# A decoder block with product-key experts: dense path moved to the middle four chunks, last selections moved into the dense loop

## Chip, cores and metric

One NeuronCore of a Trainium2 chip runs the whole kernel as one program. The metric is the device time of one execution in microseconds (us); lower is better. PE is the matrix engine, DVE the vector engine, ACT the scalar engine, POOL the GpSimd engine and SP the engine that issues most of the DMAs. The kernel is written for a planner: Python emits instructions in a program order, the planner plays them through a model of the chip and fixes from that the order of each engine's own queue. Where two instructions are ready, the one that was emitted earlier goes first. On the chip every engine then works through its queue strictly in that order.

## What is computed

A token sequence (16 meta tokens and 1024 tokens, width 1024) goes through a convolution branch beside causal attention, then through a product-key expert layer, then a final norm. Only the expert layer matters here. Per token it picks 8 x 16 of 16384 experts and mixes them:

```python
q = (xb @ wq).reshape(C, PEER_HEADS, 2, PEER_DK_HALF)
s = jnp.einsum('chpd,hpnd->chpn', q, keys).astype(jnp.float32)
sv, si = lax.top_k(s, K)                                    # 16 of 128 keys, twice per head
cand = sv[:, :, 0, :, None] + sv[:, :, 1, None, :]
cidx = si[:, :, 0, :, None] * N_KEYS + si[:, :, 1, None, :]
top_s, sel = lax.top_k(cand.reshape(C, PEER_HEADS, K * K), K)
eidx = jnp.take_along_axis(cidx.reshape(C, PEER_HEADS, K * K), sel, axis=-1)
g = jax.nn.softmax(top_s, axis=-1)
u = u_tab[eidx]
act = jax.nn.gelu(jnp.einsum('chkd,cd->chk', u, xb).astype(jnp.float32), approximate=False)
w = (g * act).astype(xb.dtype)
return jnp.einsum('chk,chkd->cd', w, v_tab[eidx])
```

## The kernel before

The 1024 tokens are 8 chunks of 128, in five sets: set 0 is chunk 0, set 1 chunk 1, set 2 chunks 2 and 3, set 3 chunks 4 and 5, set 4 chunks 6 and 7. ORDER (L61) is the program order of the middle of the kernel. B is the attention of a set (`attend`), C its output projection, expert queries and first top-16 (`mix_out`), S its second top-16 with the indices and weights (`select`), T the turning of these so that tokens lie along the free axis (`turn`), E one chunk's expansion of its weights into a table g_d in memory (`expand`), X, Y, N and U open pools, transpose the dense chunks and start the first three dense steps, G32 takes 32 gather steps, D0 is the dense loop (`dense`).

The expert layer is done in two ways. **Gathered chunks** (GATHER, 0 to 3): 128 tiles of 512 KB are fetched from u_tab (tile ug, L687, 3 buffers), each reduced on DVE against the tokens (ujunk, L690), and 128 from v_tab (tile vg, L713, 7 buffers), each four of them used by 16 matmuls (gv, L717). This makes 2 x 4 x 128 = 1024 tiles. `gather_all` runs them in rounds of steps of four tiles: u of chunk 0; then v of chunk 0 beside u of the next; and so on; v of the last alone, 160 steps in all. **Dense chunks** (DENSE, 4 to 7): 128 steps i1, each the product of 512 tokens with 128 experts (pa, 24 matmuls with split operands), Gelu, weighting by g_d (gt, L817), splitting into wh and wl, and after every four steps the product with v_tab (pv, 96 matmuls). In the dense loop 1.1 gather steps are emitted per i1 (RATE), so that v of the second gathered chunk is emitted from i1 = 29 on. The planner may take emitted work earlier when nothing emitted before it can use the engine; tile pools that are opened late (those of `dense` after the ones of `expand` and `select` are closed) hold their work back until the memory is free.

`select` is a chain between two engines: DVE makes eq (L636), POOL multiplies it into ep (L637), DVE reduces ep (L638), 16 times per chunk. `expand` is one too: DVE makes two, one and ah (L752 to L754), every second al is made by POOL (L755), PE multiplies, ACT copies out (st, L763).

Of the kernel before, what the change touches and what calls it, by code (L numbers as in the profile page):

```python
# [13 lines left out]
F32 = mybir.dt.float32  # L14
F32R = mybir.dt.float32r
# [20 lines left out]
H = 8  # L36
# [23 lines left out]

ORDER = "B1 C1 S1 B2 C2 T1 S2 B3 C3 T2 S3 B4 X0 C4 T3 E0 E1 Y0 S4 T4 E2 N0 E3 U3 G32 D0"  # L61
RATE = 1.1
CONV_POOL = [3]
GATHER = [0, 1, 2, 3]
DENSE = [4, 5, 6, 7]
ND = len(DENSE) * P
# [16 lines left out]
def trunk_kernel(ctx, tc, x, meta, g_mix, w_ab, w_lat, g_q, w_uq, g_kv, w_ukv, conv_w, conv_b,  # L83
# [468 lines left out]
    def mix_out(si, MT):  # L552
# [22 lines left out]

        sv = [sel.tile([P, H, 2, TK], F32, name=f"sv{si}_{j}", tag="sv", bufs=dim.nw) for j in range(nt)]
        sx = [sel.tile([P, H, 2, TK], U32, name=f"sx{si}_{j}", tag="sx", bufs=dim.nw) for j in range(nt)]
        for h in range(H):
# [29 lines left out]

    def select(c, sv, sx):
        si = sel.tile([P, H, 2, TK], F32, name=f"si{c}", tag="sif", bufs=1)  # L610
        V.tensor_copy(si, sx)
# [12 lines left out]
        ti = sel.tile([P, H, TK], U32, name=f"ti{c}", tag="ti", bufs=1)  # L624
        for h in range(H):
            top16(tv[:, h], ti[:, h], cand[:, h], NCAND)
        tf = sel.tile([P, H, TK], F16, name=f"tf{c}", tag="tf", bufs=1)
        V.tensor_copy(tf, ti)
        e = sel.tile([P, H, TK], F32, name=f"ef{c}", tag="ef", bufs=dim.nw)
        for h in range(0, H, HB):  # L630
            for i, n in enumerate((NC1, NCAND)):
                ks = slice(8 * i, 8 * i + 8)
                sh = [P, HB, n, 8]
                eq = sel.tile(sh, F16, name=f"eq{c}_{h}_{i}", tag=f"eq{i}", bufs=2)
                pr = sel.tile(sh, F32, name=f"ep{c}_{h}_{i}", tag=f"ep{i}", bufs=2)
                V.tensor_tensor(eq, tf[:, h:h + HB, None, ks].broadcast_to(sh), iota_c[:, None, :n].broadcast_to(sh), op=OP.is_equal)  # L636
                G.tensor_tensor(pr, eq, cidx[:, h:h + HB, :n, None].broadcast_to(sh), op=OP.mult)  # L637
                V.tensor_reduce(e[:, h:h + HB, ks], pr.rearrange("p h c k -> p h k c"), axis=AX.X, op=OP.add)  # L638
        g = sel.tile([P, H, TK], F32, name=f"gg{c}", tag="gg", bufs=dim.nw)
        gs = sel.tile([P, H], F32, name=f"gs{c}", tag="gs", bufs=1)  # L640
# [15 lines left out]
    def turn(c):  # L656

        ef, g = picks[c]
        tp = bank(f"et{c}", (P, 4, P), "s" if c in DENSE else "c")
        transpose_to(tp[:, 0], ef, P)  # L660
        eT = const.tile([P, P], I32, name=f"eT{c}", tag="eT", bufs=5)
        V.tensor_copy(eT, tp[:, 0])
        if c in GATHER:
            chunks[c] += (eT,)
        else:
            transpose_to(tp[:, 1], g.rearrange("p h k -> p (h k)"), P)
            t = sel.tile([P, 4, P], F16, name=f"gd{c}", tag="gd", bufs=len(DENSE))
            A.activation(t[:, 0], tp[:, 1], AF.Copy, scale=GSCALE)
            V.scalar_tensor_tensor(t[:, 1], tp[:, 1], GSCALE, t[:, 0], op0=OP.mult, op1=OP.subtract)
            ii = sel.tile([P, 2, P], I32, name=f"ii{c}", tag="ii", bufs=1)  # L670
            V.tensor_scalar(ii[:, 0], eT, 7, None, op0=OP.logical_shift_right)
            V.tensor_scalar(ii[:, 1], eT, NK - 1, None, op0=OP.bitwise_and)
            V.tensor_copy(t[:, 2:4], ii)
            chunks[c] = t
# [20 lines left out]
    def gather_v(c):  # L695
# [27 lines left out]
        V.tensor_tensor(ht, ht, acc, op=OP.add)  # L723
        finish(c, ht)

# [6 lines left out]

    def finish(c, ht):
        r = inv_rms(ht, f"o{c}")
        V.scalar_tensor_tensor(ht, ht, r, gfin, op0=OP.mult, op1=OP.mult)  # L735
        nc.scalar.dma_start(out[c * P:(c + 1) * P], ht)
# [49 lines left out]
    def dense_u(i1, bank):  # L786
# [9 lines left out]
        return ge  # L796

    def dense():
        dn = ctx.enter_context(tc.tile_pool(name="dn", bufs=1, **RW))
        psd = ctx.enter_context(tc.tile_pool(name="psd", bufs=1, space=PSUM, **RW))  # L800

        def pbank(name):
# [6 lines left out]
        for g in range(NK // NG):  # L809
# [3 lines left out]
            for b in range(NG):  # L813
                i1 = NG * g + b
                ge = ges.pop(0) if ges else dense_u(i1, pbank)
                gev = ge.rearrange("p (a t) -> p a t", t=TG)
                V.tensor_tensor(gev, gev, gt[:, :, b], op=OP.mult)  # L817
                wh = dn.tile([P, ND], F32R, name=f"wh{i1}", tag="wh", bufs=5)
                wl = dn.tile([P, ND], F32R, name=f"wl{i1}", tag="wl", bufs=4)
                A.activation(wh, ge, AF.Copy)  # L820
                V.tensor_tensor(wl, ge, wh.bitcast(F32), op=OP.subtract)  # L821
                W.append((wh, wl))
                while done < RATE * (i1 + 1):
                    next(steps, None)
                    done += 1
# [9 lines left out]
        for _ in steps:  # L835
            pass
        for ci, c in enumerate(DENSE):
            finish(c, acc[:, ci])

    dim = SimpleNamespace(nw=1, nk=1, wraw=WRAW0)  # L840
    al_ctx, cp_ctx, bp_ctx, ex_ctx, sel_ctx, ps_ctx = [ctx.enter_context(ExitStack()) for _ in range(6)]
# [29 lines left out]
    for t in tops[0]:  # L871
        select(*t)
        turn(t[0])
    for _ in front:
        pass
    for c_ in (bp_ctx, cp_ctx, sel_ctx, ps_ctx, al_ctx):
        c_.close()
    dim = SimpleNamespace(nw=NW, nk=NC, wraw=WRAW)
    psv = ctx.enter_context(tc.tile_pool(name="psv", bufs=1, space=PSUM, **RW))
    ps = ps_ctx.enter_context(tc.tile_pool(name="ps", bufs=1, space=PSUM, **RW))  # L880
    open_banks(ps, c=2, b=2, s=2)
    gp = ctx.enter_context(tc.tile_pool(name="gp", bufs=1, side="right", **RW))
    sel = select_pool()
    cp, gffn = mix_pool("left")
    bp, k_m, v_m, goa = attend_pool("right")
    gfin = load_bcast(gp.tile([P, D], F32, name="gfin"), g_fin)
    wd = [gp.tile([P, 4, 8 * 32], F32, name=f"wd{q}") for q in range(2)]
# [3 lines left out]
    for step in ORDER.split():  # L891
# [5 lines left out]
        elif step[0] == "S":  # L897
            for t in tops[i]:
                select(*t)
        elif step[0] == "T":  # L900
# [7 lines left out]
        elif step[0] == "Y":  # L908
            cp_ctx.close()
            dx = ctx.enter_context(tc.tile_pool(name="dx", bufs=1, **RW))  # L910
            XD = (dx.tile([P, KD, ND], F32R, name="xdh"), dx.tile([P, KD, ND], F32R, name="xdl"))
            du = ctx.enter_context(tc.tile_pool(name="du", bufs=1, **RW))
            ges = []
        elif step[0] == "N":
            dense_x()
        elif step[0] == "U":
            ges += [dense_u(k, lambda n: bank(n)) for k in range(i)]
        elif step[0] == "E":
            expand(i)
        elif step[0] == "D":  # L920
            ex_ctx.close()
            sel_ctx.close()
            ps_ctx.close()
            dense()
        else:
            for _ in range(i):
                next(steps)
# [54 lines left out]
```

## Time and profile before

| | |
|---|---|
| time, median of 3 runs | 3044.03 us (3032.12, 3044.03, 3045.99) |
| profiled execution, its own time | 3022.82 us |
| span of the profile | 3021.0 us |
| busy: PE / DVE / POOL / ACT | 86% / 71% / 52% / 33% |
| moved by DMA | 858 MB, 284 GB/s over the span |

The span is the time from the first to the last instruction; the execution's own time holds 1.8 us more. A busy share over the whole span mixes stages: the first 1400 us have many short waits between engines, the rest is the dense loop, in which PE has hardly a gap.

### The profile page before, as it was taken

The page shows a single profiled execution, that of the slowest core. Times are in us where ns is not written, and L with a number is a line of the kernel's source. Part 1 is how long each engine was busy: PE and PEld are TensorE (multiplying, and loading weights), DVE is VectorE, ACT ScalarE, POOL GpSimd, SP SyncE. Part 2 cuts the span into 40 slices and gives each one's busy share as a digit, 9 for nine tenths or more (in the row PEclk, how much of TensorE's full clock was granted, in tenths as well). Part 3 has the DMA queues.
Part 4 walks back from the last instruction along what each step waited for, and adds up shares of the span by engine and source line. Part 5 has one row for each costly group of instructions (what it writes and reads, how often), then busy time and mean ns, then how long its engine had stood idle before and what let it go on. Part 6 is the DMA issues. An engine that isn't in the chain of part 4 may idle for free. (4 is left out here: it accounts for less than half of the span.)

```text
span 3021.0 us, 40497 instructions
## 1 busy us (share of the span) xinstructions
PE 2592.5 (86%) x13295; PEld 1928.7 (64%) x13295; DVE 2158.9 (71%) x4917; ACT 1010.7 (33%) x2200; POOL 1572.4 (52%) x1608
## 2 busy tenths in 40 slices
PE   7788668897886755556999999999999999999998
PEld 6775446676653533334877777777777777776665
DVE  4789857989998999775887866666666666643333
ACT  6435425352430333342232222222222222222222
POOL 5885443534568667663343454544554445434443
PEclk9888859898898877667999999999999999999999
DMA  5014689897788996998888899999999999988996
GB/s 159 29 49 150 216 256 317 263 294 237 241 318 292 335 314 208 325 296 300 308 289 288 297 374 331 343 343 348 335 340 342 348 333 343 338 287 313 320 321 229
DMA packets 372563, 858.36 MB, mean 284 GB/s; under 512 B 37952, under 2 KB 134400, under 8 KB 368256
## 3 DMA queue, kind: packets, MB, share of 16 engines
q0 software_dynamic: 147456, 536.94, 50.8%
q1 hardware_dynamic: 216528, 295.68, 29.1%
q10 hardware_dynamic: 8368, 23.15, 2.1%
q8 instruction: 105, 1.72, 0.2%
q14 instruction: 106, 0.87, 0.1%
HBM read 798.92 MB, written 56.71 MB: 283 GB/s over the span
## 5 line engine op out<-in xcount | busy, mean ns | idle before, releaser
L713 POOL DMA_INDIRECT vg<-in_dram,eT x512 | 563.0, 1100 | 635.7 <-PE gv L717 504.3
L687 POOL DMA_INDIRECT ug<-in_dram,ei x512 | 545.5, 1065 | 605.4 <-DVE ujunk L690 328.9
L690 DVE SCALAR_TENSOR_TENSOR ujunk<-ug,xn 128x1024 bf16<-128x1024 f32 x512 | 640.6, 1251 | 144.2 <-DMA ug<-in_dram,ei 140.8
L834 DVE TENSOR_TENSOR acc<-acc,pv 128x512 f32<-128x512 f32 x256 | 171.5, 685 | 204.7 <-PE pv L178 204.2
L717 PE MATMUL gv<-vg,wd 128*32 128x512 f32 x2048 | 272.2, 649 | 24.8 <-DMA vg<-in_dram,eT 24.5
L178 PE MATMUL pv<-v_0h,wh 128*128 128x512 f32 x512 | 201.2, 398 | 26.5 <-ACT wh L820 20.1
L178 PE MATMUL pa<-xdh,u_0h 128*128 128x512 f32 x512 | 202.0, 395 | 5.6 <-ACT st L763 4.2
L178 PE MATMUL pv<-v_1l,wh 128*128 128x512 f32 x512 | 201.2, 395 | 5.5 <-DVE v_1l L783 5.5
L178 PE MATMUL pa<-xdl,u_0h 128*128 128x512 f32 x512 | 201.3, 393 | 0.0
L178 PE MATMUL pv<-v_0l,wh 128*128 128x512 f32 x512 | 201.1, 396 | 0.0
L178 PE MATMUL pa<-xdh,u_1h 128*128 128x512 f32 x512 | 201.1, 393 | 0.0
L178 PE MATMUL pa<-xdh,u_1l 128*128 128x512 f32 x512 | 200.7, 392 | 0.4 <-DVE u_1l L783 0.3
L178 PE MATMUL pa<-xdh,u_0l 128*128 128x512 f32 x512 | 200.8, 392 | 0.0
L178 PE MATMUL pa<-xdl,u_1h 128*128 128x512 f32 x512 | 200.1, 391 | 0.3 <-DVE xdl L192 0.3
L178 PE MATMUL pv<-v_1h,wl 128*128 128x512 f32 x512 | 200.0, 393 | 0.0
L782 ACT ACTIVATE u_1h<-u_1r 128x512 fp32r<-128x512 f32 x128 | 80.7, 631 | 350.4 <-PE pa L178 346.2
L178 PE MATMUL pv<-v_1h,wh 128*128 128x512 f32 x512 | 196.0, 395 | 0.0
L178 PE MATMUL pv<-v_0h,wl 128*128 128x512 f32 x512 | 194.8, 395 | 1.0 <-DVE wl L821 1.0
L763 ACT ACTIVATE st<-pg 128x256 f32<-128x256 f32 x256 | 128.6, 646 | 200.7 <-PE pg L761 157.7
L782 ACT ACTIVATE u_0h<-u_0r 128x512 fp32r<-128x512 f32 x128 | 80.8, 631 | 322.9 <-PE pa L178 320.6
L783 DVE TENSOR_TENSOR u_0l<-u_0r,u_0h 128x512 fp32r<-128x512 f32 x128 | 90.0, 703 | 118.6 <-ACT u_0h L782 114.6
L760 PE MATMUL pg<-ah,two 128*128 128x128 f16 x512 | 97.1, 269 | 82.7 <-DVE ah L754 60.2
(449 smaller groups left out, 5887.5 us busy)
## 6 DMA issues: line engine op xcount, KB each, us to landing
g_d<-st SPq DMA_DIRECT2D x32, 1024.0 KB
u_0r<-in_dram SPq DMA_DIRECT2D x128, 256.0 KB
u_1r<-in_dram SPq DMA_DIRECT2D x128, 256.0 KB
gt<-g_d SPq DMA_DIRECT2D x32, 1024.0 KB
v_0r<-in_dram SPq DMA_DIRECT2D x128, 256.0 KB
v_1r<-in_dram SPq DMA_DIRECT2D x128, 256.0 KB
wo<-in_dram SPq DMA_DIRECT2D x80, 256.0 KB
wq<-in_dram SPq DMA_DIRECT2D x80, 256.0 KB
```

Of the source, the lines that this page charges most:

```text
L178: PE.matmul(dst, l, r, start=first and j == 0, stop=last and j == 2)
L687: G.indirect_dma_start(out=ug, out_offset=None, in_=u_tab, in_offset=bass.IndirectOffsetOnAxis(ap=ei[:, j:j + 1], axis=0))
L690: V.scalar_tensor_tensor(junk, ug, 1.0, xn, op0=OP.mult, op1=OP.mult, accum_out=dots[:, j:j + 1])
L713: G.indirect_dma_start(out=vg[j], out_offset=None, in_=v_tab, in_offset=bass.IndirectOffsetOnAxis(ap=eT[:, t:t + 1], axis=0))
L717: PE.matmul(acc[32 * j:32 * j + 32, 512 * n:512 * n + 512], w[:, j, 32 * i:32 * i + 32], vg[j][:, 512 * n:512 * n + 512], start=q == 0 and ...
L760: PE.matmul(pg[:, k], two[:, a, :, b], ah[:, a, :, b], start=True, stop=False)
L763: A.activation(st[i][:, :, r0 + r:r0 + r + 4].rearrange("p a b -> p b a"), pg[:, :, i * NK // 2:(i + 1) * NK // 2], AF.Copy, scale=1.0 / G ...
L782: A.activation(hi, raw, AF.Copy)
L783: V.tensor_tensor(lo, raw, hi.bitcast(F32), op=OP.subtract)
L834: V.tensor_tensor(a, a, pv, op=OP.add)
```

## The change

Chunks 2 to 5 become the dense ones, chunks 0, 1, 6 and 7 the gathered ones. ORDER changes: the expansions E0 to E3 stand ahead of C4, and S4 and T4 are gone from it. `select` becomes a generator with eight yields; inside `dense` a generator `late_set` runs `select` and `turn` of chunks 6 and 7, one slice after each i1, so that chunk 6 is emitted by i1 = 8 and chunk 7 by i1 = 16. What these slices need gets a pool of its own (late) and a new sel pool in the dense phase, with single instead of double buffers; the turned tables gd move to the pool of `expand`; ef and gg get four buffers before the dense loop. To make room, g_final is no longer held: it is loaded into a vg buffer once for each gathered chunk and once for the dense ones, and wh has four instead of five buffers. In the dense loop `turn` takes one of the three PSUM banks of pa.

```diff
-ORDER = "B1 C1 S1 B2 C2 T1 S2 B3 C3 T2 S3 B4 X0 C4 T3 E0 E1 Y0 S4 T4 E2 N0 E3 U3 G32 D0"
+ORDER = "B1 C1 S1 T1 B2 C2 S2 B3 C3 S3 B4 X0 T2 T3 E0 E1 E2 E3 C4 Y0 N0 U3 G32 D0"
-GATHER = [0, 1, 2, 3]
-DENSE = [4, 5, 6, 7]
+GATHER = [0, 1, 6, 7]
+DENSE = [2, 3, 4, 5]
+LATE = 4
...
+        pool = late if si == LATE else sel
+        sv = [pool.tile([P, H, 2, TK], F32, name=f"sv{si}_{j}", tag="sv", bufs=dim.nw) for j in range(nt)]
...
         for h in range(H):
+            if h % 2 == 0:
+                yield
             top16(tv[:, h], ti[:, h], cand[:, h], NCAND)
+        yield
...
-        e = sel.tile([P, H, TK], F32, name=f"ef{c}", tag="ef", bufs=dim.nw)
+        e = sel.tile([P, H, TK], F32, name=f"ef{c}", tag="ef", bufs=dim.sp)
         for h in range(0, H, HB):
+            if h and h % 2 == 0:
+                yield
...
-                eq = sel.tile(sh, F16, name=f"eq{c}_{h}_{i}", tag=f"eq{i}", bufs=2)
-                pr = sel.tile(sh, F32, name=f"ep{c}_{h}_{i}", tag=f"ep{i}", bufs=2)
+                eq = sel.tile(sh, F16, name=f"eq{c}_{h}_{i}", tag=f"eq{i}", bufs=dim.sb)
+                pr = sel.tile(sh, F32, name=f"ep{c}_{h}_{i}", tag=f"ep{i}", bufs=dim.sb)
...
-        tp = bank(f"et{c}", (P, 4, P), "s" if c in DENSE else "c")
+        tp = bank(f"et{c}", (P, 4, P), "c")
...
-        finish(c, ht)
+        finish(c, ht, load_bcast(gp.tile([P, D], F32, name=f"gfin{c}", tag="vg", bufs=7), g_fin))
...
+    def late_set():
+        for t in tops[LATE]:
+            for _ in select(*t):
+                yield
+            turn(t[0])
+
     def dense():
...
+        banks["c"] = (psd, 3, "act")
+        rest = late_set()
...
-                wh = dn.tile([P, ND], F32R, name=f"wh{i1}", tag="wh", bufs=5)
+                wh = dn.tile([P, ND], F32R, name=f"wh{i1}", tag="wh", bufs=4)
...
                 W.append((wh, wl))
+                next(rest, None)
                 while done < RATE * (i1 + 1):
                     next(steps, None)
                     done += 1
...
+        gfin = load_bcast(gp.tile([P, D], F32, name="gfin", tag="vg", bufs=7), g_fin)
         for ci, c in enumerate(DENSE):
-            finish(c, acc[:, ci])
+            finish(c, acc[:, ci], gfin)
...
+    late = ctx.enter_context(tc.tile_pool(name="late", bufs=1, side="right", **RW))
...
-    gfin = load_bcast(gp.tile([P, D], F32, name="gfin"), g_fin)
...
             sel_ctx.close()
             ps_ctx.close()
+            dim.sb = dim.sp = 1
+            sel = ctx.enter_context(tc.tile_pool(name="sel", bufs=1, side="right", **RW))
             dense()
```

## Rows read from the trace of the kernel before

**Rows 1.** The page's second part: busy tenths in 40 slices of the span.

```profile
PE   7788668897886755556999999999999999999998
DVE  4789857989998999775887866666666666643333
```

**Rows 2.** Stages: each engine's busy time (instructions), granted clock, DMA share, GB/s.

```profile
1110.00:1205.00 95.00, 52.90 (x325) 33.26 (x324) 92.91 (x261) 30.82 (x59) 73.08 (x83) 0.70 0.75 249
1205.00:1395.00 190.00, 105.78 (x741) 67.14 (x739) 129.66 (x195) 71.93 (x144) 118.72 (x91) 0.64 0.92 300
1395.00:1725.00 330.00, 298.34 (x1278) 240.68 (x1280) 263.41 (x445) 93.32 (x164) 121.71 (x111) 0.96 0.86 301
1725.00:2995.00 1270.00, 1267.49 (x6213) 913.98 (x6208) 731.09 (x1176) 353.88 (x593) 603.51 (x560) 1.00 0.92 331
```

**Rows 3.** The same stages, POOL's fetches of u tiles alone (L687).

```profile
1205.00:1395.00 190.00, 37.90 (x31) 0.64 0.92 300
1395.00:1725.00 330.00, 121.20 (x110) 0.96 0.86 301
1395.00:3021.00 1626.00, 314.21 (x289) 0.99 0.90 322
```

**Rows 4.** The same, POOL's fetches of v tiles alone (L713).

```profile
1205.00:1395.00 190.00, 42.61 (x40) 0.64 0.92 300
1395.00:1725.00 330.00, 0.51 (x1) 0.96 0.86 301
1395.00:3021.00 1626.00, 409.51 (x378) 0.99 0.90 322
```

**Rows 5.** Groups by line, 1110 to 1205 us: busy, mean ns, idle before.

```profile
L638 DVE TENSOR_REDUCE ef<-ep 128x8 f32<-128x160 f32 (+1 forms) x29 | 18.3, 644 | 0.0
L636 DVE TENSOR_TENSOR eq<-tf,iota_c 128x160 f16<-128x160 f16 (+1 forms) x32 | 14.3, 470 | 0.0
L619 DVE TENSOR_TENSOR cand<-sv 128x32 f32<-128x32 f32 (+3 forms) x11 | 3.6, 393 | 0.0
L604 DVE FIND_INDEX8 ti<-tv,cand 128x8 uint32<-128x50 f32 x16 | 3.0, 196 | 0.0
...
L637 POOL TENSOR_TENSOR ep<-eq,cidx 128x160 f32<-128x160 f16 (+1 forms) x32 | 26.6, 853 | 11.4 <-DVE eq L636 11.3
...
L763 ACT ACTIVATE st<-pg 128x256 f32<-128x256 f32 x36 | 18.2, 643 | 36.6 <-PE pg L761 30.2 <-DMA g_d<-st 6.4
L795 ACT ACT_TABLE_LOAD x1 | 1.3, 1283 | 0.0
```

**Rows 6.** Groups by line, 1205 to 1395 us.

```profile
L763 ACT ACTIVATE st<-pg 128x256 f32<-128x256 f32 x136 | 68.3, 647 | 112.4 <-PE pg L761 89.1 <-DMA g_d<-st 10.9 <-DVE ht L735 6.9
...
L753 DVE TENSOR_TENSOR one<-io,gd 128x1024 f16<-128x1024 f16 x33 | 22.6, 685 | 38.4 <-POOL al L755 38.3
```

**Rows 7.** Groups by line, 1395 to 1725 us, DVE's largest.

```profile
L690 DVE SCALAR_TENSOR_TENSOR ujunk<-ug,xn 128x1024 bf16<-128x1024 f32 x111 | 135.6, 1222 | 50.5 <-DMA ug<-in_dram,ei 49.2 <-DMA xn<-xn_d 0.7
```

**Rows 8.** Waits of 1395 to 1725 us: total, times, longest.

```profile
POOL ug L687 <- DVE ujunk L690: 189.9, 95, 13.5
...
ACT wh L820 <- PE pv L178: 16.8, 5, 12.3
```

**Rows 9.** Timeline near the end, POOL and PE: start, duration, instruction, idle before.

```profile
2960.45 0.94 POOL L713 DMA_INDIRECT vg<-in_dram,eT  x1 [4.21 <-PE gv L717]
2961.70 0.95 POOL L713 DMA_INDIRECT vg<-in_dram,eT  x1 [0.30 <-issue]
...
2969.37 1.19 POOL L713 DMA_INDIRECT vg<-in_dram,eT  x1 [4.17 <-PE gv L717]
...
2976.11 1.92 PE L717 MATMUL gv<-vg,wd 128*32 128x512 f32 x16
...
3009.44 0.39 PE L178 MATMUL pv<-v_1h,wl 128*128 128x512 f32 x1
```

**Rows 10.** DMA issues: count, median us from issue to landing.

```profile
vg<-in_dram,eT POOLq DMA_INDIRECT x512, 6.3
```

More of the change, by code (lines that the diff above doesn't have):

```diff
@@ L574, in mix_out @@
             to_T(hs[j], P, NT, j * P)
-        sv = [sel.tile([P, H, 2, TK], F32, name=f"sv{si}_{j}", tag="sv", bufs=dim.nw) for j in range(nt)]
-        sx = [sel.tile([P, H, 2, TK], U32, name=f"sx{si}_{j}", tag="sx", bufs=dim.nw) for j in range(nt)]
+        pool = late if si == LATE else sel
+        sv = [pool.tile([P, H, 2, TK], F32, name=f"sv{si}_{j}", tag="sv", bufs=dim.nw) for j in range(nt)]
+        sx = [pool.tile([P, H, 2, TK], U32, name=f"sx{si}_{j}", tag="sx", bufs=dim.nw) for j in range(nt)]
         for h in range(H):
@@ L638, in select @@
                 V.tensor_reduce(e[:, h:h + HB, ks], pr.rearrange("p h c k -> p h k c"), axis=AX.X, op=OP.add)
-        g = sel.tile([P, H, TK], F32, name=f"gg{c}", tag="gg", bufs=dim.nw)
+        g = sel.tile([P, H, TK], F32, name=f"gg{c}", tag="gg", bufs=dim.sp)
         gs = sel.tile([P, H], F32, name=f"gs{c}", tag="gs", bufs=1)
@@ L666, in turn @@
             transpose_to(tp[:, 1], g.rearrange("p h k -> p (h k)"), P)
-            t = sel.tile([P, 4, P], F16, name=f"gd{c}", tag="gd", bufs=len(DENSE))
+            t = ex.tile([P, 4, P], F16, name=f"gd{c}", tag="gd", bufs=len(DENSE))
             A.activation(t[:, 0], tp[:, 1], AF.Copy, scale=GSCALE)
             V.scalar_tensor_tensor(t[:, 1], tp[:, 1], GSCALE, t[:, 0], op0=OP.mult, op1=OP.subtract)
-            ii = sel.tile([P, 2, P], I32, name=f"ii{c}", tag="ii", bufs=1)
+            ii = ex.tile([P, 2, P], I32, name=f"ii{c}", tag="ii", bufs=1)
             V.tensor_scalar(ii[:, 0], eT, 7, None, op0=OP.logical_shift_right)
@@ L731, in gather_all, with finish @@
             streams = [gather_v(c) for c in GATHER[k:k + 1]] + [gather_u(c) for c in GATHER[k + 1:k + 2]]
-    def finish(c, ht):
+    def finish(c, ht, gfin):
         r = inv_rms(ht, f"o{c}")
@@ L836, in dense @@
             pass
+        gfin = load_bcast(gp.tile([P, D], F32, name="gfin", tag="vg", bufs=7), g_fin)
         for ci, c in enumerate(DENSE):
-            finish(c, acc[:, ci])
-    dim = SimpleNamespace(nw=1, nk=1, wraw=WRAW0)
+            finish(c, acc[:, ci], gfin)
+    dim = SimpleNamespace(nw=1, nk=1, wraw=WRAW0, sb=2, sp=1)
     al_ctx, cp_ctx, bp_ctx, ex_ctx, sel_ctx, ps_ctx = [ctx.enter_context(ExitStack()) for _ in range(6)]
@@ L871, in trunk_kernel @@
     for t in tops[0]:
-        select(*t)
+        list(select(*t))
         turn(t[0])
@@ L877, in trunk_kernel @@
         c_.close()
-    dim = SimpleNamespace(nw=NW, nk=NC, wraw=WRAW)
+    dim = SimpleNamespace(nw=NW, nk=NC, wraw=WRAW, sb=2, sp=4)
     psv = ctx.enter_context(tc.tile_pool(name="psv", bufs=1, space=PSUM, **RW))
@@ L898, in trunk_kernel @@
             for t in tops[i]:
-                select(*t)
+                list(select(*t))
         elif step[0] == "T":
```

## Prediction

> **What bounds the kernel now.** Read the busy tenths first [rows 1]: PE is at 9 or more from slice 19 on, about 1395 us, and below that before. The span has two parts, and they must be costed apart.
>
> *Before 1395 us* no engine is full for long. The windows [rows 2] show DVE nearly full, 92.9 of 95 us, from 1110 to 1205 us, where `select` of chunks 6 and 7 runs, and 129.7 of 190 us after it, where only E2 and E3 are left. In that second stretch DVE waits 38.3 us for POOL's al [rows 6], which stands behind fetches in POOL's queue. This part ends when the last st is copied.
>
> *From 1395 us* PE carries the end: 298 of 330 us, then 1267 of 1270 us at a granted clock of 1.00, the upper of its two levels [rows 2]. But it does not stand alone. The gather stream runs beside it for the whole time: 289 + 378 = 667 of the 1024 tiles are fetched after 1395 us [rows 3, 4], and its last matmuls end only some microseconds before the last pv at 3009.4 us [rows 9]. So two chains end together, PE's and the gather's. A change that starts the dense loop earlier helps only as far as the gather gets as much done in the shorter time.
>
> The gather has three paces. From 1205 to 1395 us: 71 tiles in 190 us, 0.37 per us. From 1395 to 1725 us u tiles alone, 110 in 330 us, plus one v: v of chunk 1 is emitted from i1 = 29 on, and PE has older work until then. From 1725 to 2995 us the rest, 667 - 111 = 556 tiles in 1270 us, 2.28 us each [rows 2 to 4].
>
> **The change part by part.**
>
> *Out of the first part.* `select` of two chunks leaves it. DVE: eq 14.3, 32 reductions of 0.64 = 20.6, five steps of top-16 of about 3.0 each = 15, candidates twice 3.6: close to 60 us with small ones [rows 5]. POOL: 26.6 us for ep. The stretch took 95 us, but E made 36 of its 256 copies in it, and at the pace of the next stretch (136 in 190 us, 1.4 us each) these need 50 us of their own [rows 5, 6]. So at least 95 - 50 = 45 us go. At most the 95 us go: E's part of the stretch would then fit into the 60 us in which DVE is idle in the next one [rows 2]. Moving E ahead of C4 lets C4's top-16 fill that idle time in place of the fetch-bound work, so I stand nearer to the upper end: 80 us, dense loop from 1315 us.
>
> *What the gather loses by that.* 80 us at 0.37 tiles per us are 30 tiles. POOL gets 26.6 us back, at most 21 tiles at one issue per 1.25 us [rows 9]; DVE is wanted by others, so I credit 10. At 1315 us 357 - 30 + 10 = 337 tiles are done; before, at 1395 us, 1024 - 667 = 357.
>
> *Into the dense loop.* 60 us of DVE enter the first 16 or so i1, about 180 us, ahead of the u fetches in program order. DVE was 263 of 330 us busy there, and of its idle 67 us 49 were waits for a u tile to land [rows 2, 7]; POOL in turn waited 190 us for DVE to free u buffers [rows 8]. So DVE is the pace of the u stream. A u tile costs 1.22 us of DVE [rows 7]. If the select takes all its time from ujunk, 60 / 1.22 = 49 tiles go; if it fills all the idle time of those 180 us (a fifth, 37 us), 23 / 1.22 = 19 go. I take 30. In the first 330 us 111 - 30 = 81 tiles are fetched instead of 111. Single buffers of eq and ep make each of 32 hand-overs wait for POOL's queue; dense splits stand behind them on DVE, and behind those PE. That is the reason not to take 19.
>
> *PE.* Its work is the same except for some 10 more v tiles after the start: 1.92 us per four [rows 9], 5 us. Without the gather it would end at 3010 - 80 + 5 = 2935 us, less 0.48 us for each tile left to the end.
>
> *Small edits.* g_final costs 4 more loads of 512 KB and, with ht, holds a second vg buffer at each chunk's end, on SP's queue ahead of later weights: between nothing and one four-tile step (9 us, 2960.45 to 2969.37 [rows 9]) each, so 0 to 36; I take 8, since the weights are loaded ahead. One wh buffer less makes ACT wait for pv; that wait was 16.8 us in 330 before [rows 8], and ACT is busy 93 of 330 [rows 2]: 0 on the path, and if its cover goes, the splits behind wh are late by as much again. Exp between Gelus reloads tables, at most four loads of 1.3 us [rows 5] on the same idle ACT: 0. The two late turns hold one of three pa banks for a transpose: 0.
>
> *The sum.* At 1315 + 330 = 1645 us 337 + 81 = 418 tiles are done; 606 are left, with the 8 us for g_final worth 610. At 2.28 us each PE's dense work ends at 2908 us with 57 tiles left: (2908 - 1645) / 2.28 = 553, and 2935 - 57 x 0.48 = 2908. Then v tiles are fetched alone. Before, four of them took 9 us (2.28 a tile), which is what seven buffers give when a tile lands 6.3 us after its issue [rows 9, 10]: 0.95 + 6.3 + 1.92 = 9.2. Without the weights on the DMA engines they should land sooner; the issues allow 1.25 a tile. Between 1.25 and 2.28 I take 1.75: 57 x 1.75 = 100 us, to 3008. The way from the last matmul to the end took 3021.0 - 3009.8 = 11 us; 3019 us of span, 3021 us with the 1.8 us around it, against 3022.8. The median of the three runs stands 1.0070 above that execution, so 3021 becomes **3042 us**. The 80 us are real and are given back as a gather tail behind the dense work.
>
> The Trainium skill, in DMA: Bandwidth & Descriptors, Anatomy of one DMA, fits a POOL-issued transfer by 2.0 us plus its bytes over 436 GB/s. For 512 KB that is an estimate of 3.2 us to land; with it a step of four takes 6.1 us, the tail 87 us, and the median would be 3029. The row has twice that landing time, in loaded DMA; no run so far shows an unloaded one.
>
> **The rivals.**
>
> *The gather keeps pace* (chance 0.22). If the planner hurries the gather once the select is through, PE stays the only bound: 2935 + 11 + 2 = 2948, median 2969. For it: PE waits hardly ever for a v tile, while POOL waits for PE [rows 9], so the pace is partly an order written down beforehand. Against it: the DMA share is already 0.92 at 331 GB/s [rows 2], and v cannot begin for chunk 7 before its 128 u tiles are through.
>
> The skill's Perfetto Trace Analysis, Roofline, says that a core alone on its memory can draw about 120% of 358 GB/s. By that the DMA engines have room at 331, and it would be this rival's time; the share of 0.92 speaks against it.
>
> *Slower: the tail doesn't speed up* (0.20). If v tiles go on landing as late as before, the tail is 57 x 2.28 = 130 us: 2908 + 130 + 13 = 3051, median 3072, and 3110 with 49 tiles displaced. The point from which it is slower than before is (3022.8 - 13 - 2908) / 57 = 1.79 us a tile, close to what I took. For it: the 9.2 us above is landing time, not bandwidth.
>
> *The change doesn't do what it says* (0.12). If C4, now behind the four expansions, and then N0 and U3 set the start, it moves by 20 us only, 25 below my lower bound. Then 353 tiles are done at 1375 and 434 at 1705 us, 37 are left when PE ends at 2975, and the end is 2975 + 65 + 13 = 3053, median 3074.
>
> **How the numbers follow.** My forecast has 0.46, with its own range of 3000 to 3084 from the two bounds of the displaced tiles and of the tail. About 0.5% (15 us, 3029 to 3059) is what a measurement of this kernel can tell from no change. Of the 0.46 I give 0.13 to faster, 0.27 to same, 0.06 to slower; the gather that keeps pace adds 0.22 to faster; the slow tail 0.05 to same and 0.15 to slower; the unmoved start 0.04 and 0.08. So faster 0.35, same 0.36, slower 0.29. The range 2972 to 3092 leaves out most of the lower half of the first rival and the far end of the slow tail, together 0.2.
>
> **What would show it.** In the profile after, the last st lies at about 1300 us and eq and ep lie in the first 200 us of the dense loop; u fetches in that stretch are down by a fifth to a half; near the end there is a stretch without pa or pv in which only fetches and gv run, PE idle and its clock lower, some 100 us long. If gv ends with the last pv, the first rival is right; if v steps stay 9 us apart in that stretch, the second; if the first pv lies after 1370 us, the third. The prediction is wrong above all if the planner's order gives the gather another pace between 1725 and 2995 us.

## Result and profile after

The changed kernel takes 3072.11 us (median of 4 runs, 3069.63 to 3073.35), the kernel before on the same chip 3040.24 (4 runs, 3032.12 to 3045.99): ratio 1.011, 95% interval 1.0093 to 1.0126. It is slower by 1.1%. The time lies in the predicted range, but neither the forecast (no change, from a dense start 80 us earlier) nor its reason came true: the start hardly moved.

The profiled execution of after took 3073.35 us (span 3071.5), close to its median. That of before (3022.8) lies 17 us below its median, so the two spans are 50.5 us apart where the medians are 32 apart. How far one execution can lie from another shows in two kernels of the experiments below, b_cut and b_ug10, which change only the last chunk's v tiles of the kernel before: up to 2676 us PE, DVE, POOL and SP run the same sequence of instructions in all three. The copies of the expansions (st) in before, b_cut and b_ug10:

```profile
L763 ACT ACTIVATE st<-pg x256: 593/648/714, 954.2 to 1380.2; 128x256 f32<-128x256 f32 x128
L764 ACT ACTIVATE st<-pg x256: 597/644/713, 961.2 to 1395.7; 128x256 f32<-128x256 f32 x128
L766 ACT ACTIVATE st<-pg x256: 592/647/714, 971.8 to 1397.8; 128x256 f32<-128x256 f32 x128
```

The same order of instructions came 15.5 and 17.6 us later, and its first pv (1414.6 in before) 15.8 and 18.0 us later. So a time read from one profile can differ by some 20 us from that of another execution, and the times read from before's profile are early ones. The medians and the ratios stand for several executions and decide.

The stages of after, with the columns of [rows 2] (length, busy us of PE, PEld, DVE, ACT, POOL, granted clock, DMA share, GB/s):

```profile
1110.00:1205.00 95.00, 63.45 (x476) 47.98 (x475) 75.22 (x186) 39.54 (x84) 57.53 (x44) 0.86 0.92 319
1205.00:1382.00 177.00, 104.32 (x721) 68.92 (x722) 166.53 (x510) 67.68 (x138) 121.11 (x108) 0.78 0.83 278
1382.00:1725.00 343.00, 315.66 (x1351) 251.75 (x1350) 271.15 (x457) 97.63 (x172) 133.86 (x124) 0.97 0.86 295
1725.00:2990.00 1265.00, 1264.87 (x6156) 922.59 (x6155) 754.55 (x1223) 351.60 (x596) 602.12 (x554) 1.00 0.92 331
2990.00:3055.00 65.00, 30.06 (x140) 6.38 (x138) 2.04 (x3) 0.00 (x0) 23.40 (x25) 0.63 0.72 245
```

DVE did less from 1110 to 1205 us than in [rows 2] (75 for 93 us), and the stretch behind it, in which it idled 60 us before, is now nearly full (166.5 of 177 us). The last line is new: 65 us in which PE is busy for less than half of the time and DVE for 2 us.

One tile's instructions of after: count, ns (least, median, most), first and last start.

```profile
L772 ACT ACTIVATE st<-pg x256: 576/647/726, 936.7 to 1382.3; 128x256 f32<-128x256 f32 x128
L645 DVE TENSOR_TENSOR eq<-tf,iota_c x128: 218/350/2533, 371.2 to 1489.6; 128x160 f16<-128x160 f16 x64, 128x400 f16<-128x400 f16 x64
L852 DVE TENSOR_TENSOR acc<-acc,pv x256: 652/686/695, 1423.7 to 2994.8; 128x512 f32<-128x512 f32 x128
L696 POOL DMA_INDIRECT ug<-in_dram,ei x512: 932/946/2325, 389.1 to 2747.2; - x171
L726 PE MATMUL gv<-vg,wd x2048: 592/593/1064, 829.6 to 3053.2; 128*32 128x512 f32 x187
```

The last three of these in the kernel before:

```profile
L834 DVE TENSOR_TENSOR acc<-acc,pv x256: 650/686/690, 1427.6 to 3011.6; 128x512 f32<-128x512 f32 x128
L687 POOL DMA_INDIRECT ug<-in_dram,ei x512: 932/946/2017, 387.7 to 2644.3; - x171
L717 PE MATMUL gv<-vg,wd x2048: 592/592/1063, 833.4 to 3002.6; 128*32 128x512 f32 x187
```

The last copy of the expansions (st) starts at 1382.3 us; before it was 1380.2. The dense work (acc) ends 17 us earlier than before, but u fetches end 103 us later and the v sums (gv) 50.6 us later. Some 13 us of the 17 are sums that now stand behind the dense work instead of beside it: 112 of the gv matmuls start after the last acc, before none. The chain that ended last, behind the dense work of after: start, us, what.

```profile
3010.52 4.20 DMA vg<-in_dram,eT
3014.76 3.76 PE gv L726 x16
3018.66 4.21 DMA vg<-in_dram,eT
3022.91 3.77 PE gv L726 x16
3026.80 4.16 DMA vg<-in_dram,eT
3031.01 3.57 PE gv L726 x16
...
3042.80 7.79 DMA vg<-in_dram,eT
3050.62 3.69 PE gv L726 x16
```

Such steps follow each other from 2998 us on, 8.1 us each up to 3039: a fetch from its issue to its landing, then sixteen matmuls, which release the buffer that the next fetch needs. The last step takes 11.7 us, since its fetch takes 7.8; beside it SP issues the loads of ht and of g_final (3042.6 to 3044.2 us). Counted in the trace, at 1385, 1725 and 2640 us after had issued 342, 449 and 856 of its 1024 tiles, before 355, 468 and 880. So 13 of 24 tiles were lost ahead of the dense loop, 6 in its first 340 us, 5 later; at 2.03 us a tile the 24 are 49 us, about the difference of the spans. Against b_cut (351, 461 and 869) it is 9 of 13 tiles, or 26 us. The 32 us between the medians lie between the two, and in both counts most of the tiles are lost ahead of the dense loop.

Where the front lost them stands in C4. The matmuls of its output projection (op), and the transposes that turn the lists (et), from 850 to 1200 us. First the kernel before, then after:

```profile
L563 PE MATMUL op<-wo,mt x128: 379/379/793, 900.5 to 974.9; 128*128 128x256 f32 x128
L156 PE MATMUL et<-ident,ef x4: 273/304/476, 880.2 to 984.5; 128*128 128x128 f32 x4
```

```profile
L565 PE MATMUL op<-wo,mt x128: 379/379/636, 1060.0 to 1132.0; 128*128 128x256 f32 x128
L158 PE MATMUL et<-ident,ef x4: 328/402/477, 921.5 to 1059.7; 128*128 128x128 f32 x4
```

After, C4's matmuls start 0.3 us behind the last turn, 160 us later than before. Both take their result tile from the two PSUM banks of tag c, and those are handed out in written order: T2 and T3 stand ahead of C4 now, and the last turn waits for the end of S3. In the kernel before, turns of dense chunks had tag s and C4 stood ahead of them.

### The profile page after: what moved, and what is told of

Its sections match the earlier page's. It is cut to its first block, busy times and chain, and to the rows that moved or that the text cites. A ratio compares the mean times of both kernels' runs of the same rounds, so it can differ in the third digit from the quotient of the medians.

```text
span 3071.5 us, 40520 instructions
## 1 busy us (share of the span) xinstructions
PE 2606.4 (85%) x13295; PEld 1933.7 (63%) x13295; DVE 2169.8 (71%) x4917; ACT 1006.9 (33%) x2200; POOL 1586.9 (52%) x1608
## 4 chain that ended last, share of the span: by engine, by line
PE 49%; DVE 18%; DMA 11%; issue 5%; POOL 3%; ACT 1%; SPq 0%; POOLq 0%; DVEq 0%; ACTq 0%
PE pv L180 19%; PE pa L180 18%; DMA ug<-in_dram,ei 7%; PE gv L726 7%; DVE ujunk L699 5%; DVE ef L647 2%; DMA vg<-in_dram,eT 1%; DVE eq L645 1%; DVE two L761 1%; DVE ah L763 1%; PE q L586 1%; DVE one L762 1%; PE po L523 1%; POOL ug L696 1%; DMA g_d<-st 1%
## 5 line engine op out<-in xcount | busy, mean ns | idle before, releaser
L722 POOL DMA_INDIRECT vg<-in_dram,eT x512 | 575.2, 1123 | 650.0 <-PE gv L726 523.8
L726 PE MATMUL gv<-vg,wd 128*32 128x512 f32 x2048 | 288.2, 674 | 43.3 <-DMA vg<-in_dram,eT 43.1
L180 PE MATMUL pv<-v_0h,wh 128*128 128x512 f32 x512 | 201.4, 399 | 16.9 <-ACT wh L837 11.9
L769 PE MATMUL pg<-ah,two 128*128 128x128 f16 x512 | 89.3, 256 | 133.2 <-DVE ah L763 92.9
L726 PEld LDWEIGHTS gv<-vg,wd 128*32 128x32 f32 x2048 | 58.0, 118 | 186.8 <-issue 131.1
```

What stands on the lines that cost most here:

```text
L180: PE.matmul(dst, l, r, start=first and j == 0, stop=last and j == 2)
L722: G.indirect_dma_start(out=vg[j], out_offset=None, in_=v_tab, in_offset=bass.IndirectOffsetOnAxis(ap=eT[:, t:t + 1], axis=0))
L726: PE.matmul(acc[32 * j:32 * j + 32, 512 * n:512 * n + 512], w[:, j, 32 * i:32 * i + 32], vg[j][:, 512 * n:512 * n + 512], start=q == 0 and ...
L769: PE.matmul(pg[:, k], two[:, a, :, b], ah[:, a, :, b], start=True, stop=False)
```

## Experiments

All kernels together. Ratio: to before on the same chip, with its 95% interval. The other columns come from each kernel's profile: start of the last st, of the first pv, of the last acc (end of the dense work) and of the last gv (end of the gather), in us.

| kernel | median | ratio | st | pv | acc | gv |
|---|---|---|---|---|---|---|
| before | 3040.2 | 1 | 1380.2 | 1414.6 | 3011.6 | 3002.6 |
| after | 3072.1 | 1.0110 (1.0093-1.0126) | 1382.3 | 1411.0 | 2994.8 | 3053.2 |
| cut | 3004.0 | 0.9874 (0.9847-0.9902) | 1383.6 | 1411.4 | 2993.6 | 2988.3 |
| b_cut | 3021.3 | 0.9935 (0.9913-0.9958) | 1395.7 | 1430.4 | 3017.6 | 2955.4 |
| hold | 3078.9 | 1.0123 (1.0100-1.0146) | 1352.7 | 1388.3 | 2963.8 | 3060.1 |
| s4front | 3082.5 | 1.0133 (1.0105-1.0161) | 1387.0 | 1454.1 | 3074.8 | 3052.2 |
| roles | 3078.9 | 1.0170 (1.0143-1.0197) | 1440.3 | 1469.8 | 3067.3 | 3016.4 |
| t1back | 3057.2 | 1.0079 (1.0054-1.0104) | 1363.6 | 1402.7 | 2987.7 | 3037.1 |
| b_t1early | 3055.6 | 1.0088 (1.0069-1.0107) | 1414.6 | 1447.3 | 3043.9 | 3034.9 |
| rate2 | 3065.2 | 1.0109 (1.0086-1.0131) | 1384.2 | 1414.3 | 2994.2 | 3049.2 |
| bank_s | 3037.1 | 1.0008 (0.9992-1.0024) | 1358.6 | 1396.2 | 2984.5 | 3009.7 |
| both | 3037.1 | 0.9990 (0.9978-1.0002) | 1362.2 | 1393.1 | 2972.3 | 3022.2 |
| t1psv | 3037.6 | 0.9998 (0.9986-1.0011) | 1352.6 | 1383.4 | 2965.2 | 3014.5 |
| roles_s | 3031.6 | 0.9985 (0.9970-0.9999) | 1381.6 | 1418.4 | 3011.3 | 3013.0 |
| ug10 | 3024.5 | 0.9948 (0.9932-0.9965) | 1391.1 | 1418.9 | 3016.2 | 3017.4 |
| b_ug10 | 3037.9 | 0.9989 (0.9970-1.0009) | 1397.8 | 1432.6 | 3033.0 | 2993.2 |
| best7 | 3038.0 | 0.9991 (0.9974-1.0007) | 1356.4 | 1387.5 | 2969.7 | 3019.3 |
| best10 | 2991.2 | 0.9849 (0.9809-0.9890) | 1352.5 | 1383.5 | 2975.6 | 2970.3 |

The medians are of several chips, so the ratios are to be compared, not the medians. The four columns behind them are of one execution each, and before's was a quick one: against it a shift of less than some 20 us says little. An edit can also make the planner place unrelated work behind it anew.

### What sets the end: the last 32 v tiles left out

```diff
+        nq = 3 if c == GATHER[-1] else 4
-        for q in range(4):
+        for q in range(nq):
```

The changed kernel: 

> The changed kernel without the last 32 v tiles (8 steps of four) of the last gathered chunk; the rest is computed as before. Theory 'gather sets the end': in the changed kernel 33 tiles were issued or in use after PE's dense work ended at 2989 us, at 8.1 us per step; without 32 of them the time falls by about 60 us, to 3005-3015, with the last pv still at about 2989 us or a few us earlier (8 steps of 16 matmuls less, of which none lay beside pv). Rival 'the dense work sets the end and the gather only fills the order that the planner left': the last pv moves with the gather, and the time falls by less than 25 us.

The kernel before: 

> The kernel before without the last 32 v tiles of chunk 3; the rest is computed as before. Theory 'there two chains ended together': the same cut that takes 60 us from the changed kernel takes only 5 to 20 us here, because the last pv at 3009 us stands: PE saves 8 steps x 16 matmuls (15 us at full clock) and nothing else. Rival 'the gather alone bounded the kernel before too': the time falls by 40 us or more.

Without these tiles the changed kernel is some 70 us shorter (ratio 0.9874 for 1.0110), and its dense work ends where it did:

```profile
L853 DVE TENSOR_TENSOR acc<-acc,pv x256: 647/686/690, 1424.3 to 2993.6; 128x512 f32<-128x512 f32 x128
L727 PE MATMUL gv<-vg,wd x1920: 592/592/1063, 831.7 to 2988.3; 128*32 128x512 f32 x192
```

The kernel before gets only 0.65% (20 us) from the same cut, although its gather then ends 47 us earlier; that its dense work seems to end 6 us later than before's is the spread of single executions. So the gather alone sets the end of after, and before the two chains ended together.

### What the slices do: held back, and put back into the front

hold: the late lists get a dependency on ge of the fourth dense round (times zero), and the slices begin there.

```diff
-                next(rest, None)
+                if i1 == 3:
+                    for c_, sv, sx in tops[LATE]:
+                        s_ = sv.rearrange("p a b c -> p (a b c)")
+                        V.scalar_tensor_tensor(s_, ge[:, :H * 2 * TK], 0.0, s_, op0=OP.mult, op1=OP.add)
+                if i1 >= 3:
+                    next(rest, None)
```

> The changed kernel with the late selection of both chunks made to depend on ge of the fourth round of the dense loop, so that it can't lie in the front. Theory 'it was taken early': 18 of the 32 ep hand-overs lay among the expansions before 1385 us, about 60 us of DVE work with top-16 and candidates; held back, the last st comes 30 to 60 us earlier than 1382 us and the last pv 25 to 60 us earlier than 2989 us; the gather, which loses DVE in the dense loop, ends no earlier, so the time is 3055 to 3095 and the stretch with gv alone is 80 to 130 us long. Rival 'E's pace and C4 set the start': the last st moves by less than 15 us, and the time is within 15 us of 3072.

s4front: S4 and T4 behind Y0 in the order, no slices in the dense loop.

```diff
-... E0 E1 E2 E3 C4 Y0 N0 U3 G32 D0
+... E0 E1 E2 E3 C4 Y0 S4 T4 N0 U3 G32 D0
-        rest = late_set()
+        rest = iter(())
```

> The changed kernel with the selection of the last two chunks back ahead of N0 in the front, everything else as changed. Theory 'it was taken early': the 14 hand-overs that did lie in the dense loop, some 30 us of DVE, come forward; the last st at most 20 us later than 1382 us, the time within 15 us of 3072, because what the late slices give to the start is small. Rival 'the slices do what the prediction said': the last st comes 60 to 80 us later, the last pv too, and the time goes to 3090 or more.

The first two rows are of hold, the next two of s4front.

```profile
L772 ACT ACTIVATE st<-pg x256: 577/647/731, 938.5 to 1352.7; 128x256 f32<-128x256 f32 x128
L857 DVE TENSOR_TENSOR acc<-acc,pv x256: 631/685/690, 1402.5 to 2963.8; 128x512 f32<-128x512 f32 x128
```

```profile
L772 ACT ACTIVATE st<-pg x256: 578/644/729, 939.1 to 1387.0; 128x256 f32<-128x256 f32 x128
L852 DVE TENSOR_TENSOR acc<-acc,pv x256: 673/686/690, 1464.6 to 3074.8; 128x512 f32<-128x512 f32 x128
```

hold came out as the first theory had it. The slices in the changed kernel had run early: of the 32 eq of the late chunks 20 lay ahead of 1385 us. Held back, they free 30 us of the front and 31 us of the end of the dense work, and the time doesn't fall, since the gather ends no earlier (3060.1). Nothing in the program forbade the early place: the lists were ready, and the slices found their memory free.

s4front refutes my expectation that the slices give the start little. From s4front to after the last st moves by 5 us only, but the first pv by 43 and the end of the dense work by 80.0 us; from s4front to hold the first pv moves by 66 us. So what the selection is worth for the start is to be seen only against a kernel that has the rest of the change too. That the end of the dense work moves by just the 80 us of the forecast is chance: the forecast was of the start, and more than half of the selection still lay in the front. The rest of the change takes as much away: s4front is 1.3% slower than before, 40 us. So the question is what the roles and the new order do.

### The rest of the change: roles, and T1

roles: the new roles in before's order, but for T2, which stands behind C4; selection in the front.

```diff
-B1 C1 S1 T1 B2 C2 S2 B3 C3 S3 B4 X0 T2 T3 E0 E1 E2 E3 C4 Y0 N0 U3 G32 D0
+B1 C1 S1 B2 C2 T1 S2 B3 C3 S3 B4 X0 C4 T2 T3 E0 E1 Y0 S4 T4 E2 N0 E3 U3 G32 D0
```

> The changed kernel with before's order of the front (T1 behind C2, C4 ahead of the expansions, S4 T4 ahead of E2, E3 last) and the last selection back in the front: what is left of the change is that chunks 2 to 5 are dense and 6, 7 are gathered. Theory 'the order costs the front': with the order undone the last pv comes at 3000 to 3020 us and the gather ends at about 3005, as before the change; time 3025 to 3050. Rival 'the roles themselves cost it' (chunks 2, 3 have to be turned and expanded later than they could, and 6, 7 are gathered from late lists): the last pv stays at 3060 to 3075 us and the gather at 3050, time 3070 to 3095.

The dense work stayed late (3067.3) and the time too, as the rival had it, so the order isn't all. But its first st came only at 1088.2 us, 134 later than before: C4 stands ahead of T2 and T3 here, and now the turns wait for C4. Whichever stands first holds the other up. A resource shared by turns and C4 would explain that; the runs on the bank below test it.

t1back: `S1 T1 B2 C2 S2` becomes `S1 B2 C2 T1 S2` in the changed kernel. 

> The changed kernel with T1 (the transposes of chunk 1's lists) back behind C2; one step of the order moved. Theory 'T1 ahead of B2 and C2 holds up the front': C2's normalized rows come at about 600 us instead of 670, the first 900 us hold 20 to 30 us more DVE work, the last st comes 20 to 40 us earlier than 1382 us, and with it last pv and gather; time 3030 to 3055. Rival 'T1 is harmless, the expansions ahead of C4 are what costs': last st within 10 us of 1382, time within 12 us of 3072.

b_t1early: the reverse in the kernel before. 

> The kernel before with T1 moved right behind S1 as in the changed kernel; nothing else. Theory 'T1 ahead of B2 and C2 holds up the front': the last st comes 20 to 50 us later than 1380 us, the time is 3055 to 3090. Rival 'T1 is harmless': last st within 10 us of 1380, time within 10 us of 3040.

In the kernel before, T1 alone costs 0.9%: the last st comes 17 to 19 us later than in b_cut and b_ug10 (34 later than in before's quick profile). In the changed kernel undoing it gives 0.3%, with intervals that overlap, and st 19 and gather 16 us earlier: between my two theories, and no more than a hint. T1 may be the same conflict in small, with C2 behind it; t1psv tests that.

### The bank

bank_s: one line of the change undone.

```diff
-        tp = bank(f"et{c}", (P, 4, P), "c")
+        tp = bank(f"et{c}", (P, 4, P), "s" if c in DENSE else "c")
```

> The changed kernel with one line as before: the lists of dense chunks are turned in a PSUM bank of tag s again, not of tag c. Theory 'bank c': in the changed kernel C4's first op matmul (1060.0 us) follows the last turn's transpose (1059.7) at once, because both take their two banks of tag c in program order and T2, T3 stand ahead of C4; with the turns in s, C4's op starts at 900 to 960 us, C4's rows are normalized at about 1000 us (1156 in the changed kernel), the last st comes 20 to 50 us earlier than 1382 us and the last pv 20 to 60 us earlier than 2989 us; the gather, if it gains in the front, ends 10 to 30 us earlier: time 3035 to 3065. Rival 'PE's written order holds C4': op still starts within 10 us of the last turn, time within 12 us of 3072.

```profile
L565 PE MATMUL op<-wo,mt x128: 379/379/795, 927.5 to 987.8; 128*128 128x256 f32 x128
L158 PE MATMUL et<-ident,ef x3: 272/272/474, 876.1 to 1017.6; 128*128 128x128 f32 x3
L852 DVE TENSOR_TENSOR acc<-acc,pv x256: 647/686/691, 1406.6 to 2984.5; 128x512 f32<-128x512 f32 x128
L726 PE MATMUL gv<-vg,wd x2048: 592/592/1063, 826.6 to 3009.7; 128*32 128x512 f32 x187
```

The written order is that of the changed kernel, and C4 no longer waits for the turns: its matmuls start at 927.5 us, 90 us ahead of the last turn. By 1385 us 355 tiles are issued instead of 342, the gather ends 43.5 us earlier, and the whole loss of 1.1% is gone. The dense work ends only 10 us earlier, less than the theory had (20 to 60).

roles_s: the same line in roles. 

> The roles alone (chunks 2 to 5 dense, 6 and 7 gathered) in before's order, selection of 6, 7 in the front, turns of dense chunks in tag s as before. Theory 'bank c, not the roles': with the turns in c and C4 ahead of them the first st came at 1088 us; in s it comes at 950 to 1000, the last st by 1370 to 1400, the last pv by 3000 to 3025, the gather by 3015: time 3030 to 3055 (before: 3031 to 3040). Rival 'the roles cost it': last pv at 3050 or later, time 3065 or more.

Roles, then roles_s:

```profile
L772 ACT ACTIVATE st<-pg x256: 577/646/722, 1088.2 to 1440.3; 128x256 f32<-128x256 f32 x128
L772 ACT ACTIVATE st<-pg x256: 577/644/724, 962.3 to 1381.6; 128x256 f32<-128x256 f32 x128
```

By this line alone the first st falls from 1088.2 to 962.3 us and the ratio from 1.0170 to 0.9985. The roles as such cost nothing.

both: bank_s and t1back. 

> bank_s, and T1 back behind C2. Theory 'bank c' for T1 as well: C2's rows at about 600 us, C4's op at 880 to 930 us, last pv 30 to 80 us earlier than 2989 us; the gather ends 20 to 45 us earlier than 3054: time 3020 to 3050. If the gather is paced by something else than the front, it ends at 3040 or later and only the stretch with gv alone grows: time 3055 to 3070.

t1psv: bank_s, with T1 where the change put it, but in another bank.

```diff
+        if c == 1:
+            tp = psv.tile([P, 4, P], F32, name=f"et{c}", tag="gv", bufs=1)
```

> bank_s with T1 still right behind S1, but turned in the PSUM of the v sums, which nothing else uses at that time. Theory 'bank c holds up C2 behind T1': C2's op is over by about 605 us (668 in the changed kernel) as with T1 behind C2, and the time is within 10 us of the kernel with T1 moved back. Rival 'PE's written order': C2's op ends at about 668 us and the time is that of bank_s.

PE's op matmuls from 560 to 610 us (busy us and count), in bank_s and in t1psv:

```profile
560.00:610.00 50.00, 0.00 (x0) 0.64 0.65 193
```

```profile
560.00:610.00 50.00, 28.75 (x118) 0.93 0.84 264
```

T1 turns at 617 us in t1psv and at 619 in bank_s, yet in t1psv C2's matmuls are through by 610, and in bank_s the last 128 of them run from 610 to 680. So it is the bank that holds C2 and C4, not their place in the written order: with the bank out of the way, the planner puts C2's matmuls ahead of T1 in PE's queue. In time bank_s, both and t1psv are alike, though: an earlier C2 brings the dense work forward (2984.5, 2972.3, 2965.2) and not the gather (3009.7, 3022.2, 3014.5), which sets the end in all three. And bank_s against roles_s is what new order and slices do once the bank is out of the way: the first pv comes 22 us earlier, the dense work ends 27 us earlier, the gather 3, and the ratio goes from 0.9985 to 1.0008. Nothing is gained.

### The gather's pace

rate2: `RATE = 2.0`. 

> The changed kernel with RATE 2.0 instead of 1.1, so that the gather's steps are written into the program nearly twice as early against the dense rounds. Theory 'the written order paces the v fetches' (POOL waited 120 us for PE gv between 2760 and 2990 us, a step per dense round): the step distance in that stretch falls from some 9.5 us to 8, the gather ends 20 to 40 us earlier, time 3030 to 3055. Rival 'the planner places each instruction by its own clock whatever the written order, and DMA is shared anyway': the order of u and v on POOL is nearly the same, time within 12 us of 3072. Slower is possible where ujunk, written earlier, stands ahead of the splits on DVE: then PE waits for split weights and last pv is later than 3000.

The time is that of after (1.0109). From 1385 to 1725 us 124 tiles are issued for 107, from 2640 to 2990 us 133 for 143. The written order moves tiles, it adds none.

ug10: three more buffers for the last chunk's v tiles; the u tiles need them no longer.

```diff
-                    vg.append(gp.tile(..., tag="vg", bufs=7))
+                    if c == GATHER[-1] and j == 3:
+                        vg.append(gu.tile(..., tag="ug", bufs=3))
+                    else:
+                        vg.append(gp.tile(..., tag="vg", bufs=7))
```

> The changed kernel; the fourth v tile of each step of the last gathered chunk goes to one of the three buffers of the u tiles, which are free by then, so ten buffers serve 32 steps in place of seven. Theory 'seven buffers pace the v tiles': a step no longer needs the sums of the step before to issue its fourth tile; in the stretch with gv alone a step takes 5 to 6.5 us instead of 8.1, and beside the dense work the steps come closer too, so fewer than 25 v tiles are issued after 2990 us; the gather ends 15 to 40 us earlier than 3054, last pv within 10 us of 2995: time 3030 to 3058. Rival 'landing and sums pace them': a step stays at 7.5 us or more, time within 12 us of 3072.

b_ug10, the same in the kernel before: 

> The kernel before with the same three more buffers for the last chunk's v tiles. Here dense work and gather end together (3011.6 and 3003.2 us), so both theories expect little: the gather ends 0 to 30 us earlier, the last pv stays within 8 us of 3012, time within 12 us of before. If v tiles that come sooner take DMA from the weights, the last pv comes later and the time is up to 15 us longer.

best7, from t1psv: the dense chunks' g_final goes into the buffer of gt. 

> t1psv with g_final for the dense chunks loaded into the buffer of gt, which is free after the last dense round, instead of a v buffer. If the v buffer held back the end of the dense chunks, their five normalizations and stores come before the last gv and the way from the last gv to the end falls from 17 to 11 us: time 5 to 8 us less than t1psv (3037 there). If the order on ACT and DVE holds them back, 17 us stay and the time is within 4 us of t1psv.

best10, best7 and ug10 together: 

> best7 with the ten buffers of ug10. Dense work ended at 2965 us in t1psv and the gather at 3015. If the buffers pace the v tiles, the gather ends at 2975 to 3000 us: time 2995 to 3025, faster than both kernels. If landing and sums pace them, the gather stays at 3010 and the time is that of best7, 3030 to 3037.

The v tiles beside the dense work, 2760 to 2960 us: busy us and count of PE, PEld and POOL on vg, clock, DMA share, GB/s. After, best7, best10; the last two differ by the buffers alone:

```profile
2760.00:2960.00 200.00, 39.51 (x332) 8.77 (x336) 79.64 (x80) 1.00 0.86 297
2760.00:2960.00 200.00, 42.32 (x352) 9.18 (x352) 85.23 (x86) 1.00 0.88 305
2760.00:2960.00 200.00, 48.09 (x400) 10.44 (x400) 95.24 (x98) 1.00 0.94 339
```

98 tiles are issued for 86, 2.04 us each for 2.33, and the DMA engines are as full as from 1725 to 2640 us (0.94 for 0.95). From after to ug10 it is 91 tiles for 80, and from before to b_ug10 96 for 84. The seven buffers paced the v tiles, also beside the dense work. The Trainium skill has the pattern in Perfetto Trace Analysis, Optimization Strategy: a gap that repeats on the engine that should be saturated can mean too few buffers for the next tile; the steps of after's tail, with some 4.5 us of idle PE in each, agree.

ug10 makes the changed kernel faster than the one before (0.9948); in b_ug10 the gather ends 40 us ahead of the dense work and nothing is gained. In ug10 the dense work ends at 3016 us, 21 later than in after, which I had not expected. The traces account for it. Up to 2772 us PE runs the same sequence in both, and there this execution of ug10 (12.6 us above its median) is already 8 us late. Behind that PE has no gap, and only 10 gv matmuls instead of 112 are left behind the last acc: their 13 us now lie ahead of it. best7 equals t1psv: the buffer of the dense chunks' g_final costs nothing, and the 17 us from the last gv to the end stay. The gathered chunks' loads of g_final were not varied: the last fetch takes 7.6 us in best7, 7.8 in after, and what part of that they cause is not shown. best10, in the end, takes 1.5% off the kernel before:

```profile
L858 DVE TENSOR_TENSOR acc<-acc,pv x256: 649/686/691, 1397.9 to 2975.6; 128x512 f32<-128x512 f32 x128
L732 PE MATMUL gv<-vg,wd x2048: 589/592/1062, 829.8 to 2970.3; 128*32 128x512 f32 x187
```

The turns in other banks (t1psv) are worth no gain over before, the buffers alone (ug10) 0.5%, both (best10) 1.5%: each frees one of two chains that end together.

## Why the prediction failed, point by point

- **Where the bound is** was right: two chains end together (cut, b_cut), and a gather tail behind the dense work takes the gain away.
- **The start, 80 us earlier, with a floor of 45.** This is the step that failed: the first pv moved by 3.6 us against before's quick profile, and by 19 and 22 us against b_cut and b_ug10. Two things were missing. "Turns 0" looked at the two late turns and their bank in the dense loop; the same line of the diff turns all four dense chunks in tag c instead of s, ahead of C4 in written order, and it carried the whole loss of time (bank_s). And "E ahead of C4 lets C4's top-16 fill that idle time" took C4's place in the order for free; C4's matmuls started 160 us later. The 60 us of selection were sized fairly: against s4front the start comes 43 us earlier in after and 66 in hold. But the floor assumed that they leave the front, and more than half had stayed in it; hold shows what was to be had by that, some 23 to 30 us. The bank gives the start 15 us (bank_s) to 28 (t1psv). No run does both, and none has its first pv before 1383 us, where I had the dense loop from 1315; so what the rest of the 80 us would have needed stays open.
- **Tiles displaced by the late selection: 30 of 111.** In the changed kernel 6 of 113, because most of the selection lay earlier; in hold 12 (101 tiles) against before, and 3 and 9 against b_cut (110). All are below my lower bound of 19: in hold DVE is busy 303 of the 340 us from 1385, before 268, so the selection took idle time and hardly any from the fetches.
- **The pace beside the dense work: 2.28 us per tile.** Measured from 1725 to 2990 us: 550 tiles in 1265 us, 2.30 (2.25 up to 2640). Right.
- **The tail: 57 tiles at 1.75 us, 100 us.** Measured: the dense work ended at 2995 us instead of 2908, with 24 tiles still to be issued, and the last sums 59 us later; a step of four took 8.1 us, 2.03 a tile, the last step 11.7. I let the fetches come nearer to the pace of their issues; in fact the fourth tile of a step still waits for the sums of the step before, 4.2 us of fetch and 3.76 us of sums in turn. That fetch does land sooner once the weights are gone (4.2 us, [rows 10] had a median of 6.3 for all), but the sums take twice the time (3.76 for 1.92 [rows 9]). The estimate of 3.2 us by the Trainium skill (DMA: Bandwidth & Descriptors, Anatomy of one DMA) was too low by 1.0, with three other fetches under way.
- **g_final 8 us, wh 0.** g_final: for the dense chunks' buffer nothing (best7); for the gathered chunks' loads not shown. PE waited for wh 11.9 us from 1395 to 1725 us in pv; what that cost no run shows. The end behind the last matmul took 17 us in place of 11: the four dense chunks are normalized behind the last gathered one there.
- **The rivals.** The third, with chance 0.12, is nearest to what happened: a start that moves by 20 us at most, and a median of 3074 (3072.1). It had the parts less well than the sum: 37 tiles left at 2975 us and the gather's end at 3040 (24 at 2995, and 3054), in an execution as quick as before's profile. It named C4, N0 and U3 as what sets the start, and C4 was late; why it was late it didn't know. The gather kept no pace (first rival), and a tail at 2.28 us (second) was above the measured 2.03.

## What to carry to other kernels

Before a step is moved, write down every buffer tag that it takes and who comes next in that tag: a tile that waits for its input holds its bank against all that follow in written order, and a one-word change of a tag can cost more than the move gains. Where two chains end together, shorten both or none. Read the spread of one order over several executions before a shift between two profiles is explained: here it was 18 us. And an instruction that nothing ties down is put where the planner finds room; if it is to run late, give it a dependency that makes it late.

## What the runs showed of the hardware

The same 128x512 matmul on gv takes 592 ns while PE is busy and 1062 ns in the stretch with gv alone, in which the granted clock of the stretch falls to 0.63, most of it at the lower of the two levels (1.2 GHz): there PE waits some 4.5 us of each 8.1 for a fetch. best7, granted 0.62 from 2990 to 3020 us, shows it too:

```profile
L729 PE MATMUL gv<-vg,wd x112: 592/1061/1062, 2966.6 to 3019.3; 128*32 128x512 f32 x112
```

So this tail is slow twice over, by the chain and by the clock. And from 1725 to 2640 us all eighteen kernels ran at a DMA share of 0.93 to 0.95 and 335 to 344 GB/s, however their gather stood; from 2760 to 2960 us it was 0.86 to 0.88 and 297 to 305 GB/s where seven buffers held the gather back (after, best7), and 0.94 and 339 with ten (best10). Executions of one order (before, b_cut, b_ug10) part by 16 to 19 us ahead of 1205 us, where the engines wait for each other, and by no more than 23 at 1819; from there to 2676 us, where PE has hardly a gap, the distance stays the same.
